# AdaLN column tiles of the FFNs: from the shared weight buffers and SP's queue to buffers of their own, ScalarE's queue, and requests two steps ahead

## The chip, the cores and the metric

The kernel runs on one core of a Trainium2 chip. The metric is the device time of one launch in microseconds. Before the change it is 1311.38 us, the median of three runs (1308.73 to 1312.22). One further execution, taken with the hardware profiler, took 1315.82 us; its trace is what is read here.

## The reference

Two decoder layers over 256 rows of 1024 columns, float32. Each layer has three sub-layers: a SwiGLU FFN, a token mixer with four branches, and a second FFN. Before each of them x is scaled and shifted, after it a gated residual and a layer norm follow. Shift, scale and gate (adaLN) are nine vectors per layer, each a product of the condition with a 1024 x 1024 matrix.

```
cond = jax.nn.silu(c)
for l in range(DEPTH):
    mod = (cond @ ada_w[l] + ada_b[l]).reshape(-1, 3, 3, D_MODEL)
    h = 0.5 * _swiglu(x * (1 + scale) + shift, ffn_w_in[l, 0], ffn_w_out[l, 0])    # 2816 hidden columns
    x = _layer_norm(DEEPNORM_ALPHA * x + (1 + gate) * h, ln_g[l, 0], ln_b[l, 0])
    h = _hybrid_mixer(...)                                                          # sub-layer 1, mod[:, 1]
    x = _layer_norm(...)
    h = 0.5 * _swiglu(...)                                                          # sub-layer 2, mod[:, 2]
    x = _layer_norm(...)
```

## The kernel before, in words

*Stages.* The six sub-layers follow each other: FFN (l0, s0) to 198 us, mixer to 459, FFN (l0, s2) 469 to 650, FFN (l1, s0) 663 to 843, mixer to 1105, FFN (l1, s2) 1115 to 1314. Text below calls the four FFNs the first to the fourth. PE starts its matmuls at 12.4 us.

*Weights.* `load` (L248) brings a weight in tiles of 128 x 1024 float32 (512 KB). SP's queue issues the DMA into one of five `raw` buffers (L258, L259). ACT rounds the tile to `hi` (L262), DVE computes the remainder `lo = raw - hi` (L267), and the raw buffer is free again. There are six pairs of hi and lo, and six `alt` buffers of which some tiles use two. Each product then takes three matmuls: hi by hi, hi by lo, lo by hi (L286 to L288 with 256 columns, L290 to L292 with 512).

*A FFN.* There are 22 hidden blocks of 128 columns. Block f takes two weight tiles and 48 matmuls into one of two `mm` banks. `post` (L520) follows: th on ACT (L522) and DVE (L523), h on DVE (L525), the rounded hh on ACT (L531), the remainder hl on DVE (L532). h is the last reader of the bank. Two blocks and one w_out pair then give 24 down matmuls into four accumulator banks. In the first FFN the first eight blocks are computed together, column by column of the input, in all eight banks; blocks 2 to 5 use the banks that the down matmuls need afterwards, and block 5 has the fourth of them. In the other FFNs blocks 0 and 1 are computed in another form (L604 to L609) while the boundary of the sub-layer before ends.

*AdaLN.* One vector of 1024 values is made from eight column tiles of 128 x 1024 float32 (`ada_cols`, L297). DVE multiplies a tile with the condition and sums it along the row, in one instruction (L308, the `reduce`), with a short one behind it that reads the sum. `sub_steps` (L363) puts twelve steps of two tiles each (gate of this sub-layer, shift and scale of the next) into a list; the FFN's loop over hidden blocks (L618) runs a few of them after each block. The last FFN has four steps with tiles. A tile takes a `raw` buffer, and SP's queue issues it where the program has come to. The sixteen tiles for the first scale and shift are separate (`first_block`, L1121), in a buffer `big8` of which there are three; the mixers and boundaries use those three for other things.

*Order.* Each engine runs its instructions in the order that a scheduler has written when the program is built. It takes the program's order, moved by priorities (weights are 300 ahead, L257) and by its own estimate of when operands are ready. On the chip nothing overtakes on DVE or ACT: an instruction that waits holds up those behind it.

Of the kernel before, what the change touches and what calls it, by code (L numbers as in the profile page):

```python
# [11 lines left out]
F32 = mybir.dt.float32  # L12
# [44 lines left out]
RB, QB = 5, 15  # L57
# [6 lines left out]
GD = 3  # L64
# [39 lines left out]
SS = 1  # L104
PJ = 5
AFF = 3
AM = 42
ROW_M = 10

# [35 lines left out]
def trunk(ctx: ExitStack, tc: tile.TileContext, x, xT, crow, ada0, adac, adab, w_in0, w_in0x, gcol, bcol, ln_g, ln_b,  # L145
          w_in, w_out, mpair, mv0, mv12, mbrA, mbr, mwo, bgate, bforget, eye, rot, masks, out):
    nc = tc.nc
    P = 128
    cp = ctx.enter_context(tc.tile_pool(name="cp", bufs=1))
    wp = ctx.enter_context(tc.tile_pool(name="wp", bufs=3))  # L150
    ap_ = ctx.enter_context(tc.tile_pool(name="ap", bufs=2))
    sp = ctx.enter_context(tc.tile_pool(name="sp", bufs=2))
    mp = ctx.enter_context(tc.tile_pool(name="mp", bufs=1))
# [140 lines left out]

    mods = {(l, s): {} for l in range(DEPTH) for s in range(3)}

    def ada_cols(l, s, v):  # L297

        key = ("shift", "scale", "gate")[v]

        def run(c):
            if c == 0:
                mods[(l, s)][key] = ap_.tile([P, KT], F32, tag=key, bufs=2, name=key)
            t = mods[(l, s)][key]
            for n in (2 * c, 2 * c + 1):
                raw = wp.tile([P, 1024], F32, tag="raw", bufs=RB, name="raw")
                nc.sync.dma_start(raw, adac[l, s, v, n])
                nc.vector.tensor_tensor_reduce(raw, raw, cond_row, 0.5, adab_sb[:, l * 3 + s, v, n:n + 1],  # L308
                                               ALU.mult, ALU.add, accum_out=t[:, n:n + 1])

        return [lambda c=c: run(c) for c in range(4)]

    def ada_gate(l, s):

        def spread():
            ps = tp_bank()
            nc.tensor.transpose(ps[:KT, :P], mods[(l, s)]["gate"], ident)
            col = ap_.tile([KT, P], F32, tag="grow8", bufs=1, name="grow8")
            nc.scalar.copy(col, ps[:KT, :P])
            flat = dp.tile([KT, P], F32, tag="gflat", bufs=2, name="gflat")  # L320
            nc.gpsimd.dma_start(flat, col)
            G = ap_.tile([P, D], F32, tag="row", bufs=3, name="G")
            fetch_row(G, flat.rearrange("a b -> (a b)"))
            mods[(l, s)]["G"] = G

        return spread
# [18 lines left out]
    def fetch_row(dst, row):  # L345

        with tc.issue_after(held["pool"]):
            nc.gpsimd.memset(dst, 0.0)
        nc.gpsimd.dma_start(dst[0:P:32], row.partition_broadcast(4))

    def spread_row(dst):
        for h in range(SH):
            hs = slice(h * (D // SH), (h + 1) * (D // SH))
            with tc.issue_after(held["lo"]):
                nc.vector.stream_shuffle(dst[:, hs], dst[:, hs], [0] * 32)

    def both(*fs):
        def run():
            for f in fs:
                f()  # L360
        return run

    def sub_steps(l, s, nxt):  # L363

        st = mods[(l, s)]
        nx = ada_cols(*nxt, 0) + ada_cols(*nxt, 1) if nxt else [lambda: None for _ in range(8)]

        def fetch(key, row):
            st[key] = ap_.tile([P, D], F32, tag="row", bufs=3, name=key)
            fetch_row(st[key], row)  # L370

        before = {}
        for key, n, src in (("g", ROW_M if s == 1 else ROW_G, ln_g), ("b", ROW_M if s == 1 else ROW_B, ln_b)):
            before.setdefault(n, []).append(lambda key=key, src=src: fetch(key, src[l * 3 + s]))
            before.setdefault(n + GD, []).append(lambda key=key: spread_row(st[key]))
        before.setdefault(GG, []).append(lambda: ada_gate(l, s)())
        before.setdefault(GG + GD, []).append(lambda: spread_row(st["G"]))
        seq = ada_cols(l, s, 2) + nx + ([lambda: None] * (ROW_M + GD + 1 - 12) if s == 1 else [])
        return [both(*before.get(n, []), f) for n, f in enumerate(seq)]


# [112 lines left out]
    def ffn(l, s, u, nxt, steps, first=False):  # L494
# [12 lines left out]
        def hidden(f):  # L507
            k0 = N0 if f in part else 0
            w = load(w_in[fi, f, :, k0:].rearrange("p a b -> p (a b)"))
            ps = mm_bank()  # L510
            for g in range(2):
                for kt in range(k0, KT):
                    split_mm(ps[:, g * 256:(g + 1) * 256], w((kt - k0) * 256 + g * 128, 128),
                             uh[:, kt, :], ul[:, kt, :], kt == k0, kt == KT - 1)
            if f in part:
                nc.vector.tensor_tensor(part[f], part[f], ps, op=ALU.add)
                ps = part[f]
            post(f, ps[:, :256], ps[:, 256:])
# [93 lines left out]
        for f in range(f0, NF):  # L612
            hidden(f)
            if not first and f >= AFF and held["affine"]:
                held["affine"].pop(0)()
# [23 lines left out]
    def mixer(l, u, nxt, steps):  # L639
# [12 lines left out]
        def on(n, *fs):  # L652
            turns.setdefault(n, []).extend(fs)
# [323 lines left out]
        def plan():  # L977
# [27 lines left out]
            for n, piece in enumerate(held["affine"]):  # L1005
                def late(piece=piece):
                    with tc.issue_after(held["lo"]):
                        piece()
                on(AM + n, late)

# [121 lines left out]
    for l in range(DEPTH):  # L1132
        u = ffn(l, 0, u, (l, 1), sub_steps(l, 0, (l, 1)), first=l == 0)
        u = mixer(l, u, (l, 2), sub_steps(l, 1, (l, 2)))
        nxt = (l + 1, 0) if l + 1 < DEPTH else None
        u = ffn(l, 2, u, nxt, sub_steps(l, 2, nxt))
# [55 lines left out]
```

## Time and profile before

| | before |
|---|---|
| median of three runs | 1311.38 us |
| profiled execution | 1315.82 us |
| its span, first to last instruction | 1314.0 us |
| granted TensorE clock, mean | 0.998 |
| PE busy | 1265.7 us |
| DVE busy | 1036.5 us |
| ACT busy | 652.6 us |
| reduces of adaLN columns (L308) | 128, 163.9 us |
| lo remainders (L267) | 421, 508.1 us |

The busy time of an engine is the time in which it works on an instruction. The mean over the span hides that stages differ, so the rows below are taken by stretch. A stretch's row gives each engine's busy microseconds and instruction count, the granted clock, the share in which the 16 DMA engines were busy, and the rate. A DMA share of 1.03 is full. In a timeline a row has the start, the duration, the engine, the line and the operation; behind it, in brackets, stands the engine's idle time just before and what ended it. Matmuls are pipelined: one of 256 columns is shown with 0.28 us, but the next starts 0.118 us later; one of 512 columns shows 0.39 to 0.40 and the next starts 0.235 us later.

### The profile page before, as it was taken

The page shows a single profiled execution, that of the slowest core. Times are in us where ns is not written, and L with a number is a line of the kernel's source. Part 1 is how long each engine was busy: PE and PEld are TensorE (multiplying, and loading weights), DVE is VectorE, ACT ScalarE, POOL GpSimd, SP SyncE. Part 2 cuts the span into 40 slices and gives each one's busy share as a digit, 9 for nine tenths or more (in the row PEclk, how much of TensorE's full clock was granted, in tenths as well). Part 3 has the DMA queues.
Part 4 walks back from the last instruction along what each step waited for, and adds up shares of the span by engine and source line. Part 5 has one row for each costly group of instructions (what it writes and reads, how often), then busy time and mean ns, then how long its engine had stood idle before and what let it go on. Part 6 is the DMA issues. An engine that isn't in the chain of part 4 may idle for free.

```text
span 1314.0 us, 23415 instructions
## 1 busy us (share of the span) xinstructions
PE 1265.7 (96%) x9178; PEld 1175.6 (89%) x9178; DVE 1036.5 (79%) x1701; ACT 652.6 (50%) x1023; POOL 142.8 (11%) x150
## 2 busy tenths in 40 slices
PE   6999999999999999999999999999999999999997
PEld 5989888989989889998989999899989898899995
DVE  7788887888786799877698877688878768976565
ACT  4554355447564554444355444354666545554440
POOL 0130000214222000000000000012060210100000
PEclk9999999999999999999999999999999999999999
DMA  9889893756665639887548987457476655585530
GB/s 341 324 285 313 302 306 141 255 185 223 225 235 181 227 127 319 302 277 262 175 147 312 311 282 248 128 171 239 163 248 232 222 182 175 215 315 193 187 135 33
DMA packets 85847, 300.42 MB, mean 229 GB/s; under 512 B 10604, under 2 KB 12316, under 8 KB 85736
## 3 DMA queue, kind: packets, MB, share of 16 engines
q1 hardware_dynamic: 84392, 298.00, 66.3%
q8 instruction: 72, 1.18, 0.4%
q10 hardware_dynamic: 576, 0.60, 0.1%
q0 software_dynamic: 768, 0.32, 0.1%
q14 instruction: 39, 0.32, 0.1%
HBM read 297.81 MB, written 1.07 MB: 227 GB/s over the span
## 4 chain that ended last, share of the span: by engine, by line
PE 43%; issue 19%; DMA 16%; DVE 15%; ACT 5%; POOL 1%; DVEq 0%; ACTq 0%; SPq 0%; POOLq 0%
PE mm L286 9%; PE mm L287 8%; PE mm L288 8%; DVE lo L267 6%; DMA raw<-in_w_in_dram 5%; DMA raw<-in_adac_dram 5%; PE acc L290 3%; PE acc L292 3%; PE acc L291 3%; ACT hi L262 3%; DMA raw<-in_w_out_dram 3%; DVE raw L308 3%; DMA raw<-in_mpair_dram 1%; PE tp L286 1%; PE mm L290 1%
## 5 line engine op out<-in xcount | busy, mean ns | idle before, releaser
L267 DVE TENSOR_TENSOR lo<-raw,hi 128x1024 fp32r<-128x1024 f32 (+2 forms) x421 | 508.1, 1222 | 161.3 <-ACT hi L262 159.2
L262 ACT CAST hi<-raw 128x1024 fp32r<-128x1024 f32 (+1 forms) x422 | 433.8, 1040 | 322.3 <-PE mm L287 126.9
L286 PE MATMUL mm<-uh,hi 128*128 128x256 f32 x2032 | 574.7, 283 | 5.3 <-DVE h L525 3.1
L287 PE MATMUL mm<-ul,hi 128*128 128x256 f32 x2032 | 571.2, 281 | 0.0
L288 PE MATMUL mm<-uh,lo 128*128 128x256 f32 x2032 | 570.6, 281 | 0.0
L286 PEld LDWEIGHTS mm<-uh,hi 128*128 128x128 f32 x2032 | 383.0, 189 | 12.2 <-issue 5.3
L287 PEld LDWEIGHTS mm<-ul,hi 128*128 128x128 f32 x2032 | 383.5, 189 | 1.3
L288 PEld LDWEIGHTS mm<-uh,lo 128*128 128x128 f32 x2032 | 383.1, 189 | 0.3
L308 DVE CUSTOM_DVE_ANT_0 raw<-raw,cond_row,adab 128x1024 f32<-128x1024 f32 x128 | 163.9, 1292 | 47.1 <-DMA raw<-in_adac_dram 47.0
L290 PE MATMUL acc<-hi,hh 128*128 128x512 f32 x352 | 140.6, 400 | 2.2 <-ACT hh L531 1.7
L291 PE MATMUL acc<-lo,hh 128*128 128x512 f32 x352 | 139.1, 395 | 0.8 <-DVE lo L267 0.8
L292 PE MATMUL acc<-hi,hl 128*128 128x512 f32 x352 | 137.6, 396 | 0.1
L290 PEld LDWEIGHTS acc<-hi,hh 128*128 128x128 f32 x352 | 66.1, 188 | 17.7 <-ACT hh L531 3.3
L531 ACT CAST hh<-h 128x256 fp32r<-128x256 f32 x82 | 33.2, 405 | 97.4 <-DVE h L525 95.7
L292 PEld LDWEIGHTS acc<-hi,hl 128*128 128x128 f32 x352 | 65.9, 187 | 17.1 <-DVE hl L532 0.6
L291 PEld LDWEIGHTS acc<-lo,hh 128*128 128x128 f32 x352 | 66.1, 188 | 15.0 <-DVE lo L267 1.1
L408 POOL TENSOR_TENSOR rstd<-rstd,nhalf 128x1 f32<-128x1 f32 x12 | 7.6, 634 | 479.8 <-DVE rstd L407 479.8
L532 DVE TENSOR_TENSOR hl<-h,hh 128x256 fp32r<-128x256 f32 x74 | 31.2, 421 | 12.6 <-ACT hh L531 12.6
L290 PE MATMUL acc<-hi,uh 128*128 128x256 f32 (+1 forms) x128 | 38.7, 303 | 1.5 <-ACT uh L436 1.4
L1073 POOL TENSOR_TENSOR merged<-merged,tg 128x512 f32<-128x512 f32 x16 | 24.8, 1548 | 135.7 <-DVE tg L1071 57.2
L286 PE MATMUL tp<-y,hi 128*128 128x256 f32 x112 | 33.2, 297 | 5.8 <-ACT pt L753 5.7
L292 PE MATMUL acc<-hi,ul 128*128 128x256 f32 (+1 forms) x128 | 38.3, 299 | 0.0
(242 smaller groups left out, 1519.7 us busy)
## 6 DMA issues: line engine op xcount, KB each, us to landing
raw<-in_w_in_dram SPq DMA_DIRECT2D x174, 512.0 KB, 5.5
raw<-in_adac_dram SPq DMA_DIRECT2D x128, 512.0 KB, 5.4
raw<-in_mpair_dram SPq DMA_DIRECT2D x104, 512.0 KB, 4.9
raw<-in_w_out_dram SPq DMA_DIRECT2D x88, 512.0 KB, 5.3
ada<-in_ada_dram SPq DMA_DIRECT2D x16, 512.0 KB, 6.7
raw<-in_mwo_dram SPq DMA_DIRECT2D x16, 512.0 KB, 4.5
raw<-in_mv_dram SPq DMA_DIRECT2D x16, 384.0 KB, 3.8
raw<-in_mbr_dram SPq DMA_DIRECT2D x12, 512.0 KB, 3.8
```

Source lines behind the costliest of these rows:

```text
L262: nc.scalar.copy(hi[:, :half], raw[:, :half])
L267: held["lo"] = nc.vector.tensor_sub(lo[:, :half], raw[:, :half], hi[:, :half].bitcast(F32)).ins
L286: nc.tensor.matmul(ps, lhsT=wh, rhs=xh, start=start, stop=False)
L287: nc.tensor.matmul(ps, lhsT=wh, rhs=xl, start=False, stop=False)
L288: nc.tensor.matmul(ps, lhsT=wl, rhs=xh, start=False, stop=stop)
L290: nc.tensor.matmul(ps, lhsT=xh, rhs=wh, start=start, stop=False)
L291: nc.tensor.matmul(ps, lhsT=xh, rhs=wl, start=False, stop=False)
L292: return nc.tensor.matmul(ps, lhsT=xl, rhs=wh, start=False, stop=stop).ins
L308: nc.vector.tensor_tensor_reduce(raw, raw, cond_row, 0.5, adab_sb[:, l * 3 + s, v, n:n + 1], ALU.mult, ALU.add, accum_out=t[:, n:n + 1])
L531: nc.scalar.copy(hh, h)
L532: eng.tensor_sub(hl, h, hh.bitcast(F32))
L1073: eng.tensor_tensor(mg, mg, t, op=ALU.add)
```

## The change

In the FFNs (`own`) a pair of column tiles goes into one `big8` buffer, and ACT's queue issues its two DMAs. A step now asks for the pair two steps on and then reduces its own; the first step asks for three. In the mixers both tiles of a pair are asked for ahead of both reduces, otherwise as before. The line numbers of the changed kernel are higher: L267 becomes L268, L308 becomes L318, L523 becomes L546, L525 becomes L548, L532 becomes L555. 80 of the 128 tiles are in the FFNs: 24 in each of the first three, 8 in the fourth.

```diff
+AHEAD = 2
-    def ada_cols(l, s, v):
+    def ada_cols(l, s, v, own):
         key = ("shift", "scale", "gate")[v]
-        def run(c):
+        got = {}
+        def fetch(c):
+            if own:
+                two = mp.tile([P, 2, 1024], F32, tag="big8", bufs=3, name="adac")
+                got[c] = [two[:, 0], two[:, 1]]
+            else:
+                got[c] = [wp.tile([P, 1024], F32, tag="raw", bufs=RB, name="raw") for _ in range(2)]
+            for h in range(2):
+                (nc.scalar if own else nc.sync).dma_start(got[c][h], adac[l, s, v, 2 * c + h])
+        def reduce(c):
             if c == 0:
                 mods[(l, s)][key] = ap_.tile([P, KT], F32, tag=key, bufs=2, name=key)
             t = mods[(l, s)][key]
-            for n in (2 * c, 2 * c + 1):
-                raw = wp.tile([P, 1024], F32, tag="raw", bufs=RB, name="raw")
-                nc.sync.dma_start(raw, adac[l, s, v, n])
+            for h, raw in enumerate(got.pop(c)):
+                n = 2 * c + h
                 nc.vector.tensor_tensor_reduce(raw, raw, cond_row, 0.5, adab_sb[:, l * 3 + s, v, n:n + 1],
                                                ALU.mult, ALU.add, accum_out=t[:, n:n + 1])
-        return [lambda c=c: run(c) for c in range(4)]
+        return [(lambda c=c: fetch(c), lambda c=c: reduce(c)) for c in range(4)]
+    def ahead(pairs, n):
+        def step(i):
+            if i == 0:
+                for f, _ in pairs[:n]:
+                    f()
+            if i + n < len(pairs):
+                pairs[i + n][0]()
+            pairs[i][1]()
+        return [lambda i=i: step(i) for i in range(len(pairs))]
...
     def sub_steps(l, s, nxt):
-        nx = ada_cols(*nxt, 0) + ada_cols(*nxt, 1) if nxt else [lambda: None for _ in range(8)]
+        own = s != 1
+        pairs = ada_cols(l, s, 2, own) + (ada_cols(*nxt, 0, own) + ada_cols(*nxt, 1, own) if nxt else [])
+        work = ahead(pairs, AHEAD if own else 0) + ([] if nxt else [lambda: None for _ in range(8)])
...
-        seq = ada_cols(l, s, 2) + nx + ([lambda: None] * (ROW_M + GD + 1 - 12) if s == 1 else [])
+        seq = work + ([lambda: None] * (ROW_M + GD + 1 - 12) if s == 1 else [])
```

The same instructions run on DVE and PE, in another order in the FFNs; 80 DMA issues stand on ACT instead of SP. Three places show the order on DVE. A reduce is a row `ISA` that reads `cond_row`, with the row that reads its sum behind it; `lo`, `th`, `h` and `hl` are as above.

DVE, first FFN, from th of hidden block 4 to h of block 5. Before:

```order
L523 SCALAR_TENSOR_TENSOR th<-th,acc 128x256
L267 TENSOR_TENSOR lo<-raw,hi 128x1024
L525 SCALAR_TENSOR_TENSOR h<-th,acc 128x256
L523 SCALAR_TENSOR_TENSOR th<-th,acc 128x256
L525 SCALAR_TENSOR_TENSOR h<-th,acc 128x256
```

After, the stretch from behind th of block 4 to h of block 5:

```order
L318 ISA adac,shift<-adac,cond_row,adab 128x1024
L318 ISA shift 128x1
L548 SCALAR_TENSOR_TENSOR h<-th,acc 128x256
L318 ISA adac,shift<-adac,cond_row,adab 128x1024
L318 ISA shift 128x1
L268 TENSOR_TENSOR lo<-raw,hi 128x1024
L318 ISA adac,shift<-adac,cond_row,adab 128x1024
L318 ISA shift 128x1
L318 ISA adac,shift<-adac,cond_row,adab 128x1024
L318 ISA shift 128x1
L546 SCALAR_TENSOR_TENSOR th<-th,acc 128x256
L548 SCALAR_TENSOR_TENSOR h<-th,acc 128x256
```

Where one lo stood there are now one lo and four reduces. In all, h of block 5 has two lo and twelve reduces more ahead of it than before, counted from the start of the program.

DVE, second FFN, from ahead of hl of block 6 to h of block 7. Before:

```order
L532 TENSOR_TENSOR hl<-h,hh 128x256
L267 TENSOR_TENSOR lo<-raw,hi 128x1024 x3
L308 ISA raw,shift<-raw,cond_row,adab 128x1024
L308 ISA shift 128x1
L308 ISA raw,shift<-raw,cond_row,adab 128x1024
L308 ISA shift 128x1
L267 TENSOR_TENSOR lo<-raw,hi 128x1024
L523 SCALAR_TENSOR_TENSOR th<-th,mm 128x256
L267 TENSOR_TENSOR lo<-raw,hi 128x1024
L525 SCALAR_TENSOR_TENSOR h<-th,mm 128x256
```

After:

```order
L555 TENSOR_TENSOR hl<-h,hh 128x256
L318 ISA adac,scale<-adac,cond_row,adab 128x1024
L318 ISA scale 128x1
L318 ISA adac,scale<-adac,cond_row,adab 128x1024
L318 ISA scale 128x1
L268 TENSOR_TENSOR lo<-raw,hi 128x1024
L546 SCALAR_TENSOR_TENSOR th<-th,mm 128x256
L318 ISA adac,scale<-adac,cond_row,adab 128x1024
L318 ISA scale 128x1
L268 TENSOR_TENSOR lo<-raw,hi 128x1024
L548 SCALAR_TENSOR_TENSOR h<-th,mm 128x256
```

Two reduces and five lo stood between the two; now three reduces and three lo do, and the reduces are those of the next scale instead of the next shift: eight reduces that stood further back have come ahead of them. Ahead of hl of block 7 the order has three lo and eleven reduces more than before; in the third FFN three and twelve.

DVE, fourth FFN, from behind the lo remainders of blocks 0 and 1 to h of block 2. Before:

```order
L267 TENSOR_TENSOR lo<-raw,hi 128x1024 x2
L532 TENSOR_TENSOR hl<-hT,hh 128x256
L523 SCALAR_TENSOR_TENSOR th<-th,mm 128x256
L308 ISA raw,gate<-raw,cond_row,adab 128x1024
L308 ISA gate 128x1
L525 SCALAR_TENSOR_TENSOR h<-th,mm 128x256
```

After:

```order
L268 TENSOR_TENSOR lo<-raw,hi 128x1024 x2
L555 TENSOR_TENSOR hl<-hT,hh 128x256
L318 ISA adac,gate<-adac,cond_row,adab 128x1024
L318 ISA gate 128x1
L318 ISA adac,gate<-adac,cond_row,adab 128x1024
L318 ISA gate 128x1
L268 TENSOR_TENSOR lo<-raw,hi 128x1024 x3
L546 SCALAR_TENSOR_TENSOR th<-th,mm 128x256
L318 ISA adac,gate<-adac,cond_row,adab 128x1024
L318 ISA gate 128x1
L548 SCALAR_TENSOR_TENSOR h<-th,mm 128x256
```

h of block 2 now has seven lo and two reduces more ahead of it than before.

On PE the matmuls keep their places but for small ones: in the first FFN 12 matmuls of hidden block 10 stand ahead of the first 72 down matmuls, 36 behind, and the first matmul of the fourth accumulator bank is the 46th of the 72; in the second FFN four matmuls of the next hidden block stand between the two halves of a group of 24 down matmuls, in the third FFN six.

## Rows read from the trace of the kernel before

**Rows 1.** The page, part 1: busy time, share of the span, instructions.

```profile
PE 1265.7 (96%) x9178; PEld 1175.6 (89%) x9178; DVE 1036.5 (79%) x1701; ACT 652.6 (50%) x1023; POOL 142.8 (11%) x150
```

**Rows 2.** The page, part 2: busy tenths in 40 equal slices.

```profile
PE   6999999999999999999999999999999999999997
...
DMA  9889893756665639887548987457476655585530
```

**Rows 3.** Stretches: us, PE, PEld, DVE, ACT, POOL busy; clock, DMA share, GB/s.

```profile
30.00:36.00 6.00, 6.00 (x53) 6.00 (x52) 2.46 (x4) 1.90 (x4) 0.00 (x0) 1.00 1.03 407
60.00:79.20 19.20, 19.14 (x136) 17.59 (x135) 16.08 (x22) 12.30 (x20) 9.13 (x8) 1.00 0.86 280
79.20:100.00 20.80, 20.80 (x116) 17.94 (x115) 17.14 (x29) 8.47 (x16) 6.85 (x8) 1.00 0.86 293
484.00:543.00 59.00, 58.60 (x415) 54.49 (x414) 50.88 (x72) 28.01 (x37) 2.52 (x3) 1.00 0.91 322
678.00:737.00 59.00, 58.74 (x411) 54.42 (x410) 51.70 (x73) 29.24 (x40) 2.85 (x4) 1.00 0.91 323
1115.00:1142.20 27.20, 25.38 (x185) 23.21 (x184) 25.74 (x48) 13.03 (x24) 2.15 (x3) 1.00 0.47 177
145.00:198.00 53.00, 48.95 (x355) 45.19 (x354) 45.84 (x69) 26.18 (x36) 0.00 (x0) 1.00 0.91 309
600.00:650.00 50.00, 48.94 (x367) 46.53 (x367) 36.08 (x52) 23.53 (x33) 0.00 (x0) 1.00 0.68 229
795.00:843.00 48.00, 47.17 (x349) 44.63 (x349) 31.11 (x47) 22.98 (x33) 0.00 (x0) 1.00 0.67 218
```

**Rows 4.** Groups by line: count, busy us and mean ns, idle before and releasers.

```profile
L267 DVE TENSOR_TENSOR lo<-raw,hi 128x1024 fp32r<-128x1024 f32 (+2 forms) x421 | 508.1, 1222 | 161.3 <-ACT hi L262 159.2 <-PE acc L292 0.5
L308 DVE CUSTOM_DVE_ANT_0 raw<-raw,cond_row,adab 128x1024 f32<-128x1024 f32 x128 | 163.9, 1292 | 47.1 <-DMA raw<-in_adac_dram 47.0
```

**Rows 5.** Timeline, DVE, first FFN: h of block 5, reduce, h of 10.

```profile
78.77 0.42 DVE L525 SCALAR_TENSOR_TENSOR h<-th,acc 128x256 f32<-128x256 f32 x1
...
98.28 1.28 DVE L308 CUSTOM_DVE_ANT_0 raw<-raw,cond_row,adab 128x1024 f32<-128x1024 f32 x1
...
99.49 0.42 DVE L525 SCALAR_TENSOR_TENSOR h<-th,mm 128x256 f32<-128x256 f32 x1
```

**Rows 6.** Timeline, PE, first FFN: first matmul behind block 10, first of 12.

```profile
95.82 0.39 PE L290 MATMUL acc<-hi,hh 128*128 128x512 f32 x1
...
112.70 0.28 PE L286 MATMUL mm<-uh,hi 128*128 128x256 f32 x1
```

**Rows 7.** Timeline, DVE and PE, second FFN: hl of block 7, its first reader.

```profile
542.33 1.23 DVE L267 TENSOR_TENSOR lo<-raw,hi 128x1024 fp32r<-128x1024 f32 x1 [1.59 <-ACT hi L262]
543.48 0.42 DVE L532 TENSOR_TENSOR hl<-h,hh 128x256 fp32r<-128x256 f32 x1
...
544.08 0.39 PE L292 MATMUL acc<-hi,hl 128*128 128x512 f32 x1
```

**Rows 8.** Timeline, DVE and PE, third FFN: hl of block 7, its first reader.

```profile
735.79 0.42 DVE L532 TENSOR_TENSOR hl<-h,hh 128x256 fp32r<-128x256 f32 x1
...
737.01 0.40 PE L292 MATMUL acc<-hi,hl 128*128 128x512 f32 x1
```

**Rows 9.** Timeline, DVE and ACT, fourth FFN: h of block 2, end of block 3.

```profile
1141.81 0.42 DVE L525 SCALAR_TENSOR_TENSOR h<-th,mm 128x256 f32<-128x256 f32 x1
...
1147.26 0.39 ACT L522 ACTIVATE th<-mm 128x256 f32<-128x256 f32 x1 [1.33 <-PE mm L288]
```

**Rows 10.** Waits, 480 to 545 us: total, times, longest.

```profile
ACT hi L262 <- DMA raw<-in_w_in_dram: 11.8, 10, 3.0
```

**Rows 11.** DMA issues: KB and us to landing; last, one issue on ACT's queue.

```profile
raw<-in_w_in_dram SPq DMA_DIRECT2D x174, 512.0 KB, 5.5
raw<-in_adac_dram SPq DMA_DIRECT2D x128, 512.0 KB, 5.4
...
1301.07 0.35 ACTq L449 DMA_DIRECT2D out_dram<-x  x1
```

## The prediction

> **What bounds the kernel now.** I read the page's busy times first [rows 1]: TensorE (PE) is busy for 1265.7 of 1314.0 us, VectorE (DVE) for 1036.5, ScalarE (ACT) for 652.6. The reader should see that the kernel is bound by its matmuls nearly everywhere, so that little can be won and much lost. The slices [rows 2] show DMA at 8 to 9 tenths in the parts where an FFN begins (slices 1 to 6, 16 to 18, 22 to 24 and 36; a slice is 32.85 us) and at 3 to 7 nearly everywhere else. The table of stretches [rows 3] then gives what the slices cannot. In 484 to 543 us, the first half of the second FFN, PE works 58.60 of 59 us, DVE 50.88, and the DMA engines run at 0.91. The third FFN (678 to 737) is the same to a per cent. There three resources are close to their ends together, and DVE, which serves both the column sums of adaLN and the chain that feeds PE, has 8.1 and 7.3 us free. PE's own holes late in the FFNs are 4.05 (145 to 198), 1.06 (600 to 650) and 0.83 us (795 to 843): together 5.9 us, and this is all that better supply could win there.
>
> The tightest chain is the one from a hidden block to the down matmuls: tanh on ACT, th and h on DVE, the rounded half hh on ACT, the remainder hl on DVE. In the second FFN hl of hidden block 7 starts at 543.48 and takes 0.42, so it ends at 543.90; the first matmul that reads it starts at 544.08 [rows 7]. That is 0.2 us of slack. In the third FFN hl ends at 736.21 and is read at 737.01 [rows 8]: 0.8 us.
>
> **The change part by part.** Bytes, sums and matmuls stay as they are. 80 of the 128 column tiles (24 in each of the first three FFNs, 8 in the last) move from the raw buffers to buffers of their own, and their issues from SP's queue to ACT's. A step of adaLN now asks for pairs 0, 1 and 2 when it first runs, and later for the pair two steps on.
>
> *Issues.* An issue costs ACT 0.35 us [rows 11], so 24 of them cost 8.4 us in an FFN. ACT is busy 28.01 of 59 us in the stretch [rows 3], with hi casts waiting 11.8 us for w_in tiles alone [rows 10], so I take 0 for them as busy time. An issue that waits on ACT for a buffer still in use holds up all hi casts and hh copies behind it, and through hh the down matmuls. The trace of before has no such wait. Its bounds: 0, and per wait the 3.0 us of the longest wait of a hi cast on a w_in tile [rows 10]. I take 0, because the buffer is freed by DVE and the delay then is the DVE delay counted below, and keep the rest for the range.
>
> *SP.* The weights no longer stand behind 80 column tiles and keep all five raw buffers. That is the gain: at most the 5.9 us of holes. I take half, 3 us, since no row says which hole was a late weight.
>
> A tile lands 5.4 or 5.5 us after its issue from SP, whichever tensor it is from [rows 11], and the DMA engines are at 0.91 of full use in the stretches that matter [rows 3]. The Trainium skill, in "DMA: Bandwidth & Descriptors", section "Issuing engines are not separate DMA queues", says that transfers asked for by different engines run on the same 16 DMA engines and interleave, and that a second issuing engine saves only the time of issuing. By that rule the move to ACT's queue is worth nothing in transfer time and would leave 0 of the 3 us; the trace shows nothing against it.
>
> *Order on DVE.* This is the term that decides. DVE runs its instructions in a fixed order, and with the tiles asked for earlier, the column sums (reduces) stand earlier in it. I counted lo remainders and reduces ahead of each h and hl, before and after; the fences of the change show three of the places. One lo moves the next instruction by 1.15 us (542.33 to 543.48 [rows 7]), one reduce by 1.21 us (98.28 to 99.49 [rows 5]). What DVE had free up to that point is taken off, as if every tile were there in time.
>
> First FFN, h of hidden block 5: 2 more lo and 12 more reduces, 2 x 1.15 + 12 x 1.21 = 16.8 us, less 19.2 - 16.08 = 3.1 free [rows 3]: 13.7 us late, so 92.9 instead of 79.2 (78.77 + 0.42 [rows 5]). It frees the fourth accumulator bank. 45 of the 72 down matmuls of the first group can run before that, and then 27 at 0.235 and 36 of block 10 at 0.118 are left: 92.9 + 6.3 + 4.2 = 103.4, where block 10 ended at about 96 [rows 6]. h of block 10: 10 more lo and 16 more reduces, 30.9 us, less 3.1 and 20.8 - 17.14 = 3.7: 24.1 late, so 124.0 instead of 99.9. It frees the bank in which block 12 starts, at 112.70 before [rows 6]: 11.3 us late. These two delays overlap, and the larger counts: +11.3.
>
> Second FFN, hl of block 7: 3 lo and 11 reduces more, 16.8 us, less 8.1 free: 8.7 late. The slack is 0.2, and four matmuls of the next block, now between the two halves of the down group, add 0.5: +8.0. The 24 reduces are done by block 8 instead of block 14, so nothing is behind it afterwards, but PE had no idle time to make it good.
>
> Third FFN, same place: 3 lo and 12 reduces, 18.0 us, less 7.3: 10.7 late; slack 0.8, and six matmuls (0.7) between: +9.2.
>
> Fourth FFN (8 tiles only), h of block 2: 7 lo and 2 reduces, 10.5 us, less 27.2 - 25.74 = 1.5 [rows 3]: 9.0 late, 1151.2 instead of 1142.2. Block 4 takes its bank when block 3 ends, at 1147.2 [rows 9]: +4.0.
>
> Sum: 11.3 + 8.0 + 9.2 + 4.0 = 32.5, less 3.0, is 29.5 us. The profiled execution took 1315.82 us, 1.8 beyond its span, so 1345.3 on that basis. It lies 4.4 above the median of the runs, so I predict 1341 us.
>
> Bounds of the terms: should DVE's order cost nothing beyond PE's own slack, each is 0; should the transfers, not DVE, set the pace, they are those of the second rival.
>
> **Rivals.** *Faster: the weights gain.* The reduces come early only where DVE would have waited, hl and h stay in time, and the five raw buffers carry the weights further ahead: the 5.9 us of holes go, 1311.4 - 5.9 = 1305.5. It speaks for it that DVE waited 47.0 us for column tiles in the whole program [rows 4]; against it, DVE's free time before block 7 is 8.1 us, and the reduces pulled ahead of it take 13.3. It would decide if under 8 us of work stood newly ahead of hl.
>
> *Slower still: the transfers set the pace.* By block 7 of the second FFN 14 more tiles must have landed. At the best rate seen (407 GB/s [rows 3], 512 KB in 1.29 us) that is 18.0 us, less the 0.09 x 59 = 5.3 us that were free: 12.7, less 0.7 slack, +12.0 instead of +8.0. The third: 15 x 1.29 = 19.3 - 5.3 - 1.5 = +12.5. The first, up to block 10: 26 x 1.29 = 33.5, less 0.14 x 40 = 5.6, is 27.9 instead of 24.1: +15.1. The fourth stays +4.0. Less 3.0 that is 40.6, or 1352. At the 322 GB/s of the stretch itself a tile costs 1.63 us: +24.0, +16.8, +17.6, +4.0, less 3.0 is 59.4, or 1371. For it: a DMA share of 0.91 with DVE often waiting. Against it: at the boundary ahead of the second FFN (slice 15, 460 to 493 us) the engines are at 3 tenths [rows 2], and some of these tiles can land there. The Trainium skill's page named above, section "Queues, rings and completion order", has each DMA engine turn between the queues that it has work for; by that, column tiles on a queue of their own would also delay weights that SP had asked for first.
>
> *No change.* The lo remainders run many tiles ahead of PE (six pairs of hi and lo, and more in the alternate buffers), and if the order holds most of its bunching inside that lead, DVE delays tiles that nobody waits for yet, and the terms fall under PE's slack: 1311. Against it: h and hl have no such lead [rows 7, 8].
>
> **How the numbers follow.** DVE's order decides: 0.55, around 1341, by itself 1322 to 1358 (two terms of four gone, or half of the second rival's excess and the waits of ACT on top). The transfers: 0.25, 1345 to 1371. No change: 0.10. The weights gain: 0.10. A change under 0.3%, 3.9 us, cannot be told from none here. The range 1311 to 1368 leaves out the gain (0.10), the lower half of no change (0.05) and the top of the transfers (0.04). Faster 0.10, same 0.10, slower 0.80.
>
> **What would show it.** Right: PE gets a hole of 7 us or more before the first full down group and block 12 of the first FFN, 6 to 12 us around blocks 5 to 8 of the second and third, 3 to 6 before block 4 of the last, each released by DVE's h or hl (or ACT's hh behind them), with reduces back to back on DVE just before, and DVE hardly idle until there. The mixers keep their lengths. If DVE instead sits waiting for adac tiles in front of those h, the transfers are the cause; if ACT's queue sits at an issue, its waits are. The forecast is wrong if DVE's order is bunched as counted and PE shows no such holes, which would mean that h and hl have more lead than the two rows say.

## The result, and the profile after

The changed kernel takes 1385.09 us (median of four runs, 1383.19 to 1389.1) against 1311.8 for the kernel before on the same chips: 1.057 of it, 95% interval 1.0541 to 1.0599. The forecast was 1341 us, 1311 to 1368. The direction held, the size did not: 73 us instead of 30.

Below, lengths of stages come from one profiled execution each, cut where DVE first reads the accumulators at a stage's end (L401 before, L424 after). The profiled execution of before is 4.4 us above its median, and in e8 a first FFN with an unchanged order came out 4.2 us apart from the change's, so differences of a few microseconds in one stage are not to be leaned on. "Holes" are the times by which one matmul starts more than 0.3 us later after the one ahead of it than the usual step (0.118 us for 256 columns, 0.235 for 512); "slow steps" are excesses of 0.05 to 0.3 us.

| us longer than before | FFN 1 | mixer | FFN 2 | FFN 3 | mixer | FFN 4 |
|---|---|---|---|---|---|---|
| forecast (DVE's order) | 11.3 | 0 | 8.0 | 9.2 | 0 | 4.0 |
| measured | 25.1 | -0.3 | 18.0 | 21.1 | -2.3 | 11.7 |
| holes, before to after | 4.8 to 21.7 | | 3.6 to 16.6 | 2.5 to 18.4 | | 2.2 to 11.6 |
| slow steps, before to after | 1.2 to 9.9 | | 1.5 to 6.6 | 1.5 to 6.4 | | 1.3 to 3.5 |

The page after, its head and parts 1, 2, 5 and 6, in the lines that answer to [rows 1, 2, 4, 11]:

```profile
span 1387.3 us, 23402 instructions
...
PE 1290.2 (93%) x9178; PEld 1193.5 (86%) x9178; DVE 1042.9 (75%) x1701; ACT 654.9 (47%) x1023; POOL 144.1 (10%) x150
...
DMA  9998653765775639945539955537576655665540
...
L287 PE MATMUL mm<-uh,hi 128*128 128x256 f32 x2032 | 580.2, 286 | 34.7 <-DVE h L548 32.7
...
L318 DVE CUSTOM_DVE_ANT_0 adac<-adac,cond_row,adab 128x1024 f32<-128x1024 f32 x80 | 104.3, 1312 | 30.7 <-DMA adac<-in_adac_dram 30.7
...
raw<-in_w_in_dram SPq DMA_DIRECT2D x174, 512.0 KB, 5.0
...
adac<-in_adac_dram ACTq DMA_DIRECT2D x80, 512.0 KB, 6.9
```

DVE and ACT are as busy as before to a per cent; the work is the same. PE now stands 32.7 us at the first matmul of hidden blocks, waiting for h, against 3.1 before. DVE stands 30.7 us at reduces whose tile has not landed. Such waits need not cost anything: before it stood 47.0 us at them in all, 15.9 of them in the FFNs, but none ahead of the five places that the prediction prices.

A column tile of the FFNs lands 6.9 us after its issue instead of 5.7 (the 5.4 of [rows 11] is over all 128 tiles), a w_in tile 5.0 instead of 5.5. The longer landing does not come with ACT's queue. In e1 below SP's queue issues the same tiles into the same buffers:

```profile
adac<-in_adac_dram SPq DMA_DIRECT2D x80, 512.0 KB, 7.2
```

In e9, on ACT's queue but in the shared buffers, it is 5.7 again. It goes with the buffers of their own; no run says why.

The waits of DVE and ACT after, total, times and longest; the hi casts of w_in tiles waited 85.0 us before:

```profile
DVE adac L318 <- DMA adac<-in_adac_dram: 30.7, 20, 4.5
...
ACT hi L263 <- DMA raw<-in_w_in_dram: 36.1, 29, 4.3
```

So the weights are not later than before; they wait to be used.

The prediction's step can be read directly: how late DVE comes to the places it prices, how much work stands newly ahead, and how much DVE idles up to there. Stretches of DVE from the stage's start to hl of block 7 (second and third FFN) and to h of block 2 (fourth), three rows before, three after; brackets aside, the fifth number is DVE's busy time, and the second less the fifth is its idle time:

```profile
469.25:543.48 74.23, 72.54 (x526) 67.70 (x525) 65.36 (x102) 37.22 (x54) 4.68 (x6) 1.00 0.75 266
663.32:735.79 72.47, 71.20 (x517) 66.54 (x516) 64.25 (x100) 36.56 (x53) 4.67 (x6) 1.00 0.76 265
1115.13:1141.81 26.68, 24.86 (x182) 22.73 (x181) 25.22 (x47) 12.77 (x23) 2.15 (x3) 1.00 0.46 175
...
494.07:586.33 92.26, 76.87 (x530) 70.92 (x529) 81.20 (x127) 40.19 (x58) 5.81 (x8) 0.95 0.81 297
706.11:802.77 96.66, 79.59 (x528) 72.57 (x527) 81.94 (x130) 39.10 (x57) 5.79 (x8) 0.91 0.79 285
1176.73:1217.69 40.96, 30.69 (x225) 28.07 (x223) 35.68 (x56) 20.07 (x30) 2.14 (x3) 0.98 0.68 255
```

| us, at | FFN 1, h of block 5 | FFN 1, h of block 10 | FFN 2, hl of block 7 | FFN 3, hl of block 7 | FFN 4, h of block 2 |
|---|---|---|---|---|---|
| late, forecast | 13.7 | 24.1 | 8.7 | 10.7 | 9.0 |
| late, measured | 26.6 | 41.1 | 18.0 | 24.2 | 14.3 |
| more DVE work ahead, forecast | 16.8 | 30.9 | 16.8 | 18.0 | 10.5 |
| more DVE work ahead, measured | 20.6 | 34.6 | 15.8 | 17.7 | 10.5 |
| DVE idle ahead, before to after | 17.2 to 23.1 | 20.8 to 27.3 | 8.9 to 11.1 | 8.2 to 14.7 | 1.5 to 5.3 |

In the first FFN the idle time is counted from the start of the program, elsewhere from the stage's start. The work was counted to within a microsecond in three places of five and 4 us too low in the first FFN. The idle time, which the prediction took as used up, grew everywhere: up to hl of block 7 the waits for hi casts fall from 7.8 to 4.0 and from 7.0 to 2.8 us, but 6.1 and 11.0 us of waits for column tiles come on top, where there were none.

How a hole is made is best read in the fourth FFN, where the sum was simplest. The timeline of DVE after, from the last lo before the first hl to h of block 2, the place of [rows 9]:

```profile
1203.14 1.22 DVE L268 TENSOR_TENSOR lo<-raw,hi 128x1024 fp32r<-128x1024 f32 x1 [1.83 <-ACT hi L263]
1204.29 0.42 DVE L555 TENSOR_TENSOR hl<-hT,hh 128x256 fp32r<-128x256 f32 x1
1204.62 1.28 DVE L318 CUSTOM_DVE_ANT_0 adac<-adac,cond_row,adab 128x1024 f32<-128x1024 f32 x1
...
1205.82 2.36 DVE L268 TENSOR_TENSOR lo<-raw,hi 128x1024 fp32r<-128x1024 f32 x2
...
1208.85 1.29 DVE L318 CUSTOM_DVE_ANT_0 adac<-adac,cond_row,adab 128x1024 f32<-128x1024 f32 x1 [0.33 <-DMA adac<-in_adac_dram]
...
1211.54 1.28 DVE L318 CUSTOM_DVE_ANT_0 adac<-adac,cond_row,adab 128x1024 f32<-128x1024 f32 x1 [1.40 <-DMA adac<-in_adac_dram]
...
1212.75 3.49 DVE L268 TENSOR_TENSOR lo<-raw,hi 128x1024 fp32r<-128x1024 f32 x3
1216.16 0.41 DVE L546 SCALAR_TENSOR_TENSOR th<-th,mm 128x256 f32<-128x256 f32 x1
1216.49 1.28 DVE L318 CUSTOM_DVE_ANT_0 adac<-adac,cond_row,adab 128x1024 f32<-128x1024 f32 x1
...
1217.69 0.41 DVE L548 SCALAR_TENSOR_TENSOR h<-th,mm 128x256 f32<-128x256 f32 x1
```

And PE there, the last matmul of block 3 and the first of block 4:

```profile
1210.74 0.28 PE L289 MATMUL mm<-uh,lo 128*128 128x256 f32 x1
1218.16 0.58 PE L287 MATMUL mm<-uh,hi 128*128 128x256 f32 x1 [7.14 <-DVE h L548]
1218.54 0.42 PE L288 MATMUL mm<-ul,hi 128*128 128x256 f32 x1
1218.76 0.41 PE L289 MATMUL mm<-uh,lo 128*128 128x256 f32 x1
```

The forecast for this hole was 4.0 us, with DVE never idle. It is 7.3. DVE stood 5.3 us up to this h, 1.83 + 0.33 + 1.40 of them in these rows, for the hi cast of a weight and for two column tiles. Block 3 also ended 2.2 us later after the stage's start than before: 4.0 + 5.3 - 2.2 = 7.1. The hole of the third FFN has a single longer wait; DVE after, and PE after, around block 4:

```profile
744.08 1.28 DVE L318 CUSTOM_DVE_ANT_0 adac<-adac,cond_row,adab 128x1024 f32<-128x1024 f32 x1 [3.93 <-DMA adac<-in_adac_dram]
...
745.29 3.49 DVE L268 TENSOR_TENSOR lo<-raw,hi 128x1024 fp32r<-128x1024 f32 x3
748.70 0.41 DVE L546 SCALAR_TENSOR_TENSOR th<-th,mm 128x256 f32<-128x256 f32 x1
...
749.63 0.41 DVE L548 SCALAR_TENSOR_TENSOR h<-th,mm 128x256 f32<-128x256 f32 x1
```

```profile
742.23 0.27 PE L289 MATMUL mm<-uh,lo 128*128 128x256 f32 x1
750.10 0.58 PE L287 MATMUL mm<-uh,hi 128*128 128x256 f32 x1 [7.60 <-DVE h L548]
750.48 0.41 PE L288 MATMUL mm<-ul,hi 128*128 128x256 f32 x1
750.70 0.41 PE L289 MATMUL mm<-uh,lo 128*128 128x256 f32 x1
```

These holes before block 4 are the largest of their FFNs (5.3 and 7.6 us of waiting in the second and third). They are released by h of block 2, ahead of which the order has 7 lo and 1 reduce more in both; the prediction priced that place in the fourth FFN alone.

The second price is in the last rows: behind a hole matmuls start 0.21 us apart. The stretches after show the granted clock there, hole and then recovery, in the second, third and fourth FFN:

```profile
529.40:535.00 5.60, 0.31 (x4) 0.10 (x2) 5.60 (x9) 1.11 (x2) 0.00 (x0) 0.85 0.90 312
535.00:542.00 7.00, 7.00 (x40) 7.00 (x41) 5.41 (x10) 1.34 (x4) 1.72 (x3) 0.63 1.02 417
742.20:750.00 7.80, 0.30 (x3) 0.10 (x1) 5.92 (x9) 1.33 (x2) 0.00 (x0) 0.68 0.91 328
750.00:757.00 7.00, 6.90 (x39) 6.90 (x40) 7.00 (x14) 0.89 (x3) 2.52 (x3) 0.63 0.99 365
1210.70:1218.00 7.30, 0.32 (x3) 0.11 (x1) 6.46 (x9) 1.67 (x3) 0.00 (x0) 0.87 1.03 388
1218.00:1224.00 6.00, 5.84 (x31) 5.84 (x32) 6.00 (x13) 1.10 (x3) 2.45 (x3) 0.59 0.70 264
```

The third number from the end is the clock, 1.00 throughout in [rows 3]. It falls while PE stands (0.85, 0.68, 0.87). After each of the three holes it stands at 0.59 to 0.63 of 2.4 GHz in the mean of the stretch (part of it at 1.2 GHz), and 21 to 24 slow steps cost 2.2 to 2.4 us.

### The profile page after: what moved, and what is told of

It is laid out like the page before. It is cut to its first block, busy times and chain, and to the rows that moved or that the text cites. A ratio compares the mean times of both kernels' runs of the same rounds, so it can differ in the third digit from the quotient of the medians.

```text
span 1387.3 us, 23402 instructions
## 1 busy us (share of the span) xinstructions
PE 1290.2 (93%) x9178; PEld 1193.5 (86%) x9178; DVE 1042.9 (75%) x1701; ACT 654.9 (47%) x1023; POOL 144.1 (10%) x150
## 4 chain that ended last, share of the span: by engine, by line
PE 48%; issue 19%; DMA 14%; DVE 14%; ACT 4%; POOL 1%; SPq 0%; DVEq 0%; ACTq 0%; POOLq 0%
PE mm L287 10%; PE mm L288 10%; PE mm L289 10%; DVE lo L268 6%; DMA adac<-in_adac_dram 4%; PE acc L293 4%; PE acc L291 4%; DMA raw<-in_adac_dram 4%; PE acc L292 4%; DMA raw<-in_w_out_dram 3%; DMA raw<-in_w_in_dram 2%; ACT hi L263 2%; DVE raw L318 1%; DVE adac L318 1%; PE mm L291 1%
## 5 line engine op out<-in xcount | busy, mean ns | idle before, releaser
L268 DVE TENSOR_TENSOR lo<-raw,hi 128x1024 fp32r<-128x1024 f32 (+2 forms) x421 | 508.5, 1223 | 213.9 <-ACT hi L263 210.1
L287 PE MATMUL mm<-uh,hi 128*128 128x256 f32 x2032 | 580.2, 286 | 34.7 <-DVE h L548 32.7
L287 PEld LDWEIGHTS mm<-uh,hi 128*128 128x128 f32 x2032 | 388.2, 191 | 44.0 <-DVE h L548 31.7
L288 PEld LDWEIGHTS mm<-ul,hi 128*128 128x128 f32 x2032 | 388.4, 191 | 2.9 <-DVE ul L364 1.2
L289 PEld LDWEIGHTS mm<-uh,lo 128*128 128x128 f32 x2032 | 387.8, 191 | 1.3 <-DVE lo L268 1.0
L291 PE MATMUL acc<-hi,hh 128*128 128x512 f32 x352 | 146.3, 416 | 13.3 <-ACT hh L554 7.8
L292 PE MATMUL acc<-lo,hh 128*128 128x512 f32 x352 | 144.2, 410 | 0.0
L318 DVE CUSTOM_DVE_ANT_0 adac<-adac,cond_row,adab 128x1024 f32<-128x1024 f32 x80 | 104.3, 1312 | 30.7 <-DMA adac<-in_adac_dram 30.7
L318 DVE CUSTOM_DVE_ANT_0 raw<-raw,cond_row,adab 128x1024 f32<-128x1024 f32 x48 | 62.5, 1309 | 29.5 <-DMA raw<-in_adac_dram 29.5
L292 PEld LDWEIGHTS acc<-lo,hh 128*128 128x128 f32 x352 | 69.3, 197 | 14.7
L555 DVE TENSOR_TENSOR hl<-h,hh 128x256 fp32r<-128x256 f32 x74 | 31.2, 421 | 16.6 <-ACT hh L554 16.6
```

The lines of the kernel that those rows point to most:

```text
L268: held["lo"] = nc.vector.tensor_sub(lo[:, :half], raw[:, :half], hi[:, :half].bitcast(F32)).ins
L287: nc.tensor.matmul(ps, lhsT=wh, rhs=xh, start=start, stop=False)
L288: nc.tensor.matmul(ps, lhsT=wh, rhs=xl, start=False, stop=False)
L289: nc.tensor.matmul(ps, lhsT=wl, rhs=xh, start=False, stop=stop)
L291: nc.tensor.matmul(ps, lhsT=xh, rhs=wh, start=start, stop=False)
L292: nc.tensor.matmul(ps, lhsT=xh, rhs=wl, start=False, stop=False)
```

## The experiments

The order theory is the forecast's: DVE's time in reduces and lo remainders ahead of h and hl. The transfer theory is its rival: tiles and weights share the DMA engines. Each ratio is against the kernel before on the same chip.

**e1: SP's queue, all else of the change kept.**

```diff
-                (nc.scalar if own else nc.sync).dma_start(got[c][h], adac[l, s, v, 2 * c + h])
+                nc.sync.dma_start(got[c][h], adac[l, s, v, 2 * c + h])
```

> The change with one part undone: buffers of their own and the requests two steps ahead stay, but SP's queue issues the column tiles. DVE's order is then near that of before (second FFN, ahead of hl of block 7: 1 lo and 2 reduces more; third: 1 and 7; first, ahead of h of block 10: 5 lo more, 5 reduces fewer). Order theory (the loss comes from reduces that stand ahead of h and hl on DVE): the third FFN pays 1.15 + 7 x 1.21 - 7.3 - 0.8 = 1.5 us, the others nothing, 1308 to 1314 us. Transfer theory (the loss comes from tiles on a second queue that take the weights' share of the DMA engines): one queue again, 1308 to 1316 us. If buffers and early requests cost time by themselves, whatever the queue: 1345 us or more.

Measured: 1325.21 us, 1.0109 (1.0083 to 1.0134). Both ranges were missed by some 10 us, but 60 of the 73 us are gone: the queue is the larger part of the change. By stages: -5.2, +5.3, +11.1, +3.3 in the four FFNs. DVE waits 14.4 us for own tiles. That the first FFN gains 5.2 shows that something was to be had there.

**e2: reduces held back on DVE.**

```diff
+                with tc.issue_after(held["h"][-2]) if own and len(held.get("h", ())) >= 2 else ExitStack():
                     nc.vector.tensor_tensor_reduce(raw, raw, cond_row, 0.5, ...)
```

> The change with its order on DVE undone and all else kept: a reduce of an FFN may not stand ahead of h of the hidden block before the last one finished (an ordering edge behind that h). Ahead of h and hl there are then 2 to 6 reduces fewer than in the kernel before. Order theory: no holes, 1303 to 1312 us. Transfer theory: three pairs are still asked for on ACT's queue at the start of each FFN, 6 x 1.29 = 7.7 us of transfer beside the weights, and the chains have under 2 us of slack there, so about 6 us and a slow clock behind it in each FFN: 1330 to 1345 us.

Measured: 1333.56 us, 1.016 (1.0122 to 1.0197); the transfer theory's range. With the reduces held back 22 us stay, 10.4 of them in the first FFN (lo remainders still stand earlier, 5 ahead of h of block 10). DVE waits for no own tile. In the first FFN it is the weights that come late: between 56 and 76 us hi casts wait 9.9 us for them, 3.1 before. DVE of this run there, ahead of an h (PE has a hole of 4.4 us at 66.3):

```profile
64.94 1.53 DVE L268 TENSOR_TENSOR lo<-raw,hi 128x1024 fp32r<-128x1024 f32 x1 [3.43 <-ACT hi L263]
68.72 1.23 DVE L268 TENSOR_TENSOR lo<-raw,hi 128x1024 fp32r<-128x1024 f32 x1 [2.25 <-ACT hi L263]
69.86 0.41 DVE L547 SCALAR_TENSOR_TENSOR th<-th,mm 128x256 f32<-128x256 f32 x1
70.31 0.42 DVE L549 SCALAR_TENSOR_TENSOR h<-th,mm 128x256 f32<-128x256 f32 x1
```

**e3: the same tiles, reduces of 64 columns.**

```diff
+                w = 64 if own else 1024
-                nc.vector.tensor_tensor_reduce(raw, raw, cond_row, 0.5, ...)
+                nc.vector.tensor_tensor_reduce(raw[:, :w], raw[:, :w], cond_row[:, :w], 0.5, ...)
```

> The change, but the reduces of the FFNs sum 64 of the 1024 columns (the rest of the adaLN products of the FFN steps is left out). All tiles are transferred in full, at the same places on ACT's queue; DVE's order stays nearly as bunched in the first FFN (ahead of h of block 10: 10 lo and 13 reduces more than before), less in the second (ahead of hl of block 7: 1 and 6). Order theory: the 80 reduces take next to no time, only the lo remain, 10 x 1.15 - 6.8 = 4.7 us late at block 10 of the first FFN against 12.8 of slack: 1306 to 1313 us. Transfer theory: DVE still waits for the tiles ahead of h (30.7 us of such waits in the changed kernel): 1345 to 1375 us.

Measured: 1352.62 us, 1.0319 (1.0284 to 1.0354), as the transfer theory had it. Taking DVE's time for the reduces away brings 32.5 us (1385.1 to 1352.6); 41 stay. Its waits of DVE:

```profile
DVE adac L319 <- DMA adac<-in_adac_dram: 81.7, 40, 4.9
```

81.7 us instead of 30.7: DVE comes to the reduces sooner and stands there longer, with h behind it. So the 32.5 us are not the price of the reduces' work: 81 us of DVE's work went, and 51 us of it came back as waits.

**e4: the same reduces, tiles of 64 columns.**

```diff
-                (nc.scalar if own else nc.sync).dma_start(got[c][h], adac[l, s, v, 2 * c + h])
+                w = 64 if own else 1024
+                (nc.scalar if own else nc.sync).dma_start(got[c][h][:, :w], adac[l, s, v, 2 * c + h, :, :w])
-                nc.vector.tensor_tensor_reduce(raw, raw, cond_row, 0.5, ...)
+                nc.vector.tensor_tensor_reduce(raw, cond_row if own else raw, cond_row, 0.5, ...)
```

> The change, but 64 of the 1024 columns of each FFN column tile are transferred, and the reduces take the condition row twice at full width (the adaLN products of the FFN steps are replaced by a constant). DVE's work stays; its order is less bunched than in the change (first FFN, ahead of h of block 10: 10 lo and 9 reduces more than before; second, ahead of hl of block 7: 1 and 3). Order theory, with the sum of the prediction: 10 x 1.15 + 9 x 1.21 - 6.8 - 12.8 = 2.8 us in the first FFN, nothing elsewhere: 1308 to 1316 us. Transfer theory: the weights have the DMA engines to themselves: 1303 to 1309 us. Above 1330 us neither holds.

Measured: 1318.08 us, 1.0043 (1.0017 to 1.0069); some 2 us above the order theory's range. The first FFN is 2.4 us longer, where the sum of the prediction gave 2.8. DVE waits 2.6 us for a tile in all. Here the idle time ahead of hl of block 7 does shrink, from 8.9 to 4.3 and from 8.2 to 5.2 us in the second and third FFN, as the prediction took it. DVE's order moved with this edit, so e3 and e4 don't add up to the whole, and part of e4's gain is the lesser bunching.

**e5: reduces held back as in e2, SP's queue as in e1.**

> Both parts undone that the first runs charge: SP's queue issues the tiles, and reduces are pinned behind h of the block before the last; own buffers stay. The first FFN of the run with SP's queue was 5.2 us shorter than before, with 0.8 us of holes instead of 4.8. Order and transfers: the first FFN gains 5 us again, the others lose nothing: 1304 to 1310 us. If the lo remainders that have moved ahead (5 more ahead of h of block 2) cost by themselves in FFNs two to four, as the holes there in that run could mean: 1312 to 1320 us.

Measured: 1310.96 us, 0.9996 (0.9981 to 1.001): no difference from before, and between the two ranges. The first FFN gains 4.8 us, the second and third keep their times (-0.3, +0.2), the fourth loses 3.2 in the one profiled execution.

**e6: SP's queue and own buffers in the first FFN only.**

```diff
-        own = s != 1
+        own = (l, s) == (0, 0)
```

(and SP's queue as in e1.)

> Own buffers and SP's queue in the first FFN alone; the others keep the shared buffers, and their order is that of before. If the 5.2 us gained in the first FFN are its own and nothing behind it waits for what it left undone: 1311.2 - 5.2 = 1306, 1303 to 1309 us. If the mixer behind it gives them back: 1309 to 1313 us.

Measured: 1308.34 us, 0.9966 (0.9949 to 0.9983), in the range, the fastest kernel here. The first FFN is 5.5 us shorter, the rest about as before. Its stretch that answers to the 4.05 us of holes in [rows 3]:

```profile
145.00:192.00 47.00, 47.00 (x353) 44.83 (x352) 41.93 (x67) 21.19 (x31) 0.00 (x0) 1.00 0.80 297
```

PE has no hole left. The whole gains 2.9 us in the median, less than the stage, which is taken against a profiled execution of before that was itself a long one.

**e7: ACT's queue, reduces held back, requests too.** `AHEAD = 1`, each reduce behind h of the block just finished, and:

```diff
+                with tc.issue_after(held["hh"][-3]) if own and len(held.get("hh", ())) >= 3 else ExitStack():
                     (nc.scalar if own else nc.sync).dma_start(got[c][h], adac[l, s, v, 2 * c + h])
```

> ACT's queue and own buffers, reduces pinned behind h of the block just finished, and now the requests too: a DMA issue may not stand ahead of hh of two blocks earlier, one pair ahead instead of two. So the burst of three pairs at the start of an FFN is gone. Transfer theory: the holes of the pinned run (22 us in all) came from that burst: 1306 to 1318 us. If a second queue costs whenever it is used, by sharing or by issues that block ACT: 1325 to 1338 us.

Measured: 1317.83 us, 1.0049 (1.003 to 1.0068). With ACT's queue and all own buffers, 67 of the 73 us are gone. The waits of DVE for own tiles in this run:

```profile
DVE adac L320 <- DMA adac<-in_adac_dram: 0.2, 1, 0.2
```

**e8: filled holes.** 40 matmuls that nobody reads, between hidden blocks 3 and 4 of FFNs two to four.

```diff
+            if f == 4 and not first:
+                dummy = tp_bank()
+                with tc.issue_after(held["mm"]):
+                    for _ in range(DUM):
+                        warmed = nc.tensor.matmul(dummy[:, :256], lhsT=uh[:, 0, :128], rhs=uh[:, 0, :], start=True, stop=True).ins
```

> The change, with 40 matmuls that nobody reads (256 columns, 4.7 us) put between hidden blocks 3 and 4 of FFNs two to four, where PE has holes of 5.5, 7.8 and 7.3 us. Behind each of these holes some 24 matmuls start 0.212 us apart instead of 0.118, 2.2 to 2.4 us in all. If these slow matmuls are paid on top of the holes: three times 2.3 us less, 1376 to 1381 us. If DVE decides the next step anyway, so that the slow matmuls lie in time that PE has: 1383 to 1388 us. If filling is not hidden in the holes: above 1390 us.

Measured: 1379.21 us, 5.9 less than the change, though PE does 14 us of matmuls more; in the range for a clock that is paid on top. The slow steps of FFNs two to four fall from 16.5 to 8.8 us. It does not prove the price of the clock. In the profiled execution the three FFNs are 1.4, 7.8 and 2.6 us shorter, and the largest gain is where DVE's order moved (third FFN, 2 lo and 10 reduces more ahead of hl of block 7 instead of 3 and 12). The first FFN, with nothing added and the same order on all engines, came out 4.2 us longer.

**e9: ACT's queue, the five shared buffers.**

```diff
-            if own:
+            if False:
                 two = mp.tile([P, 2, 1024], F32, tag="big8", bufs=3, name="adac")
```

> One part of the change alone: ACT's queue issues the FFN column tiles, but they take the five shared raw buffers, as before. DVE's order moves less than in the change (first FFN, ahead of h of block 10: 4 lo and 6 reduces more than before; second and third, ahead of hl of block 7: 2 lo fewer and 3 reduces more). Order theory: 4 x 1.15 + 6 x 1.21 - 6.8 = 5.1 us late against 12.8 of slack, nothing elsewhere: 1308 to 1315 us. Transfer theory: a tile can only be asked for when a shared buffer is free, so at most five of 512 KB are under way in all, and no burst comes on top of the weights: 1308 to 1318 us. If a second queue takes its toll whatever the buffers (shares, or issues that wait on ACT ahead of hi casts): 1325 us or more.

Measured: 1360.91 us, 1.0369 (1.034 to 1.0399); only the alternative of a toll whatever the buffers had this. The runs show two other reasons. The first is the change's own: up to hl of block 7 DVE stands 10.1 and 11.1 us at column tiles in the second and third FFN and comes 11.1 and 12.3 us late, with 2 lo fewer and 4 reduces more ahead. The second is late weights: hi casts wait 102.9 us for w_in tiles, 85.0 before and 36.1 in the change. Tiles and weights take the raw buffers in turn, and SP's queue stands at a buffer until a reduce has let it go, whose tile ACT has asked for in its own time. SP's queue and ACT in the second FFN (480 to 580 us) of this run:

```profile
SPq L260 <- DVE gate L318: 18.8, 4, 10.1
SPq L260 <- DVE shift L318: 18.2, 4, 7.9
```

```profile
ACT hi L263 <- DMA raw<-in_w_in_dram: 25.2, 15, 6.2
```

SP stood up to 10.1 us at a buffer that a reduce held, 4.0 at most before (484 to 600 us). So the own buffers are not what costs; without them ACT's queue costs 50 us. How these divide between the two reasons is not shown.

**e10: e7 with the reduces left free.**

```diff
-                with tc.issue_after(held["h"][-1]) if own and len(held.get("h", ())) >= 1 else ExitStack():
+                with ExitStack():
```

> ACT's queue and own buffers; only the requests are held (no DMA issue of a column tile ahead of hh of two blocks earlier, one pair ahead), the reduces are left free. DVE's order comes out nearly as before by that alone (ahead of hl of block 7 of the second and third FFN 1 lo more and no reduce; of h of block 10 of the first 7 lo more, 2 reduces fewer). If the free requests are the root of both the bunched order and the burst of transfers: as in the run with both held, 1310 to 1321 us. If the reduces, left free, still stand in front of h and wait there for their tiles: 1325 to 1345 us.

Measured: 1351.31 us, 1.0304 (1.0267 to 1.0342), above both ranges. No reduce more stands ahead of hl of block 7 than in the kernel before, and yet it loses 41 us. The waits of DVE:

```profile
DVE adac L320 <- DMA adac<-in_adac_dram: 67.3, 29, 4.8
```

This run tells the count of reduces from the place of a reduce: what hurts is a reduce that stands in front of h before its tile is there.

## Why the prediction was wrong

- **The step that failed** is "less what DVE had free up to that point, as if every tile were there in time". It took DVE's idle time as usable and a reduce's price as 1.21 us. On the chip the scheduler put the reduces where their tiles had not landed, and DVE stood there, h behind it: 30.7 us in the change, 81.7 in e3, 67.3 in e10, against 0.2 in e7, where reduces stand behind h and only 6.5 us are lost. At the five places DVE's idle time did not go to nothing but grew by 2.2 to 6.5 us, and DVE came 5.3 to 17.0 us later than forecast. In the first three FFNs the waits for tiles (6.1 to 11.0 us) are as large as that growth or larger. They are not all of it: in e1, third FFN, 1 lo and 7 reduces more make hl of block 7 9.4 us late, with DVE's idle time at 8.8 us instead of 8.2, and only 2.6 of it at tiles. I had made order and transfers rivals, with 0.55 and 0.25. They are terms of one sum: an engine in fixed order pays the instruction and the wait in front of it.
- **The order term**, as work, was counted right: 15.8, 17.7 and 10.5 us against 16.8, 18.0 and 10.5, too low by 4 us in the first FFN. That e3 takes 32.5 us away and the sum was 32.5 is luck: by stages e3 stands 6.0, 11.9, 8.6 and 9.1 us under the change, forecast 11.3, 8.0, 9.2 and 4.0, and in e3 the waits grow as the work goes.
- **Its own signs.** The prediction said that DVE would be hardly idle ahead of the late h, and that DVE waiting for adac tiles there would speak for the transfers. Both came at once: the largest holes are released by h as it said, and DVE waits in front of that h. The sharing of the DMA engines that the rival priced is another matter, see the next point.
- **The transfer rival** named the wrong victim in most places. It had the DMA engines full and the weights late. In the change hi casts wait less for w_in tiles than before (36.1 us, not 85.0); the column tiles are late. Its top, 1371 us, is still 14 us short. In e2 weights are late in the first FFN, and there the rival holds.
- **What neither had** is the clock. Slow steps take 26.4 us in the four FFNs instead of 5.5; these 21 us are in no term. Holes take 55.2 us more (68.3 less 13.1), and the two, less 2.6 us that the mixers are shorter, are the 73. e8 fills three holes and is 5.9 us faster, but DVE's order moved with it, so what the clock alone costs is not shown.
- **The gain** of up to 5.9 us, of which I took 3, is real but only on SP's queue: e6 has 5.5 in the first FFN's profile and 2.9 in the median. On ACT's queue it is nowhere to be seen.
- **ACT's issues** take 0.335 us each. That they are hidden, and what waits on ACT at issues for a free buffer cost, was not isolated; in e7, which has the same 80 issues, all costs together are 6.5 us.
- **"Two steps ahead" does nothing.** With `AHEAD` 0 or 1 and nothing held back the written order of all engines is the same word for word, so it is not the diff's lookahead that sets where a request stands. I take it that the scheduler moves a request up to where a buffer is free. I read the diff's lookahead as the cause of the early reduces. e1 shows that it is the queue: behind SP's weights the same code gives an order near that of before.
- The page of the Trainium skill that I had against the change ("DMA: Bandwidth & Descriptors", section "Issuing engines are not separate DMA queues") allowed no gain in transfer time from a second issuing engine. The runs agree: a column tile in its own buffer lands 7.2 and 7.1 us after an issue from SP's queue (e1, e5) and 6.9 and 7.3 from ACT's (the change, e7). Nor is the whole faster: e5 and e7 differ in the queue, in the held requests and slightly in where the reduces stand, and the one on ACT's queue is the slower (1310.96 and 1317.83 us).
- Slips: behind the second pair of order fences I wrote that three lo stand there after; the rows show two. The sums use the counts from the program's start (3 and 11) and don't change. The counts that the expectations of e1, e3, e4 and e9 give for hl of block 7 are those ahead of h of that block; ahead of hl in the second FFN they are 0 lo and 3 reduces, 2 and 7, 0 and 4, and 2 lo fewer and 4 reduces more.

Settled by the runs: the queue is the larger part of what places reduces early (e1); holding both back restores nearly all (e7), holding one does not (e2, e10). Not settled: how the 41 us of e3 divide between DVE's waits, late weights and clock, since each edit also moved the order.

## What to carry to other kernels

When work moves to another queue, compare the written order of the engine that consumes it, and for every instruction that now stands in front of a critical one add two things: its duration, and the time until its operand lands. A load that comes earlier is no help if its consumer comes earlier still; fix the consumer's place behind the critical instruction. An engine's idle time may be taken off only if its waits can end earlier. Where PE is nearly always busy, price a hole of some microseconds with the slow matmuls behind it as well.

## What had not been expected of the hardware

After holes of 5.5 to 7.8 us matmuls of 256 columns started 0.21 us apart instead of 0.118, for 21 to 24 of them, 2.2 to 2.4 us each time. The granted clock then read 0.59 to 0.63 over the next 6 to 7 us.

A column tile of 512 KB took as long to land from ACT's queue as from SP's: 6.9 and 7.2 us in buffers of their own (the change, e1), 5.7 and 5.7 in the shared ones (e9, before).
